# One transformer block with sparse attention on one core: order of the first loads, rows of x kept on chip, index masks of tiles 2 and 3 placed beside tiles 0 and 1, one VectorE operation in a search step

## The chip, the core and the metric

The kernel runs on one core of a Trainium2 chip. The core has five engines, each with an instruction queue of its own: TensorE (matrix products and transposes, into the accumulator banks called PSUM), VectorE, ScalarE and GpSimd (element-wise work), and SyncE, which here only issues DMA transfers between DRAM and the on-chip memory. The metric is the device time of one execution in microseconds (us). Several executions are made and their median is taken; one more is recorded by the profiler, and all rows shown come from that one.

## What is computed

The reference is one block on a sequence of 1024 tokens with 1024 features, in float32: `x = x + mixer(norm(x))`, then a cross attention to 256 memory tokens, then a squared-ReLU MLP with 4096 hidden features, each added to x. The mixer is the part that the change touches:

```python
proj = h @ w_in                      # 1024 x 1752: c_q, c_kv, k_idx, w_idx, q_nsa, kv_nsa, g_nsa
q_d = _rope(_rms_norm((c_q @ w_dsa_uq)...), pos)         # 8 heads of 64
q_i = _rope((c_q @ w_idx_q)..., pos)                     # 8 index heads of 64
...
def step(args):                      # one tile of 128 queries
    idx_score = einsum('bqhs,bqh->bqs', relu(einsum('bqhd,bsd->bqhs', qi, k_i)), wi)
    idx_score = where(pos <= t, idx_score, -inf)
    _, sel = lax.top_k(idx_score, 256)                   # 256 keys for each query
    ...                              # o_dsa: attention over the selected keys
    ...                              # o_nsa: compressed, block-selected and window attention, gated
    return concatenate([o_dsa, o_nsa])
o = lax.map(step, xs); return o @ w_out
```

With 1024 tokens there are 16 blocks of 64 and 16 are selected, so the block-selected branch is plain causal attention. For the first two query tiles all earlier keys are within the 256, so they need no index mask; tiles 2 to 7 need one each.

## The kernel before

**Stages.** The sequence is cut into 8 row tiles of 128, and the projections into two parts of four tiles (`PARTS`). The *head* projects part 0 (`project(p1, 0, ...)`). Then the *main stage* runs two streams side by side: `attend`, the attention of tiles 0 to 7, and `fill`, which first projects part 1 in the pool `p2`, then prepares the memory keys and values, then takes finished tiles through `w_out`, the cross attention (`between`) and the MLP of tiles 0 to 3 (`mlp`). A *tail* does what is left and the MLP of tiles 4 to 7 (`mlp_tail`). `together` mixes the two streams by amounts of work, in a ratio from `PACES`; tile 4 may start only when part 1 is projected. Within this program order a scheduler, run when the kernel is built, chooses the order of each engine's queue from its own estimate of times. Each engine then works its queue in that order.

**Head.** Constants come first: identity, cosine and sine tables, gains, masks, the position stack `pe` (`pe_stack`, L1143). Then `project` (L371) loads the gain of norm1 (`gain`, L338) and, tile by tile, the rows of x (L378). `norm_T` (L285) squares a tile on ScalarE with a sum, takes the root on GpSimd, scales on VectorE (L290), transposes on TensorE in groups of four (L277), and copies the result out as a high and a low half (L238, L239), or as one in part 1 (L281, L283). `gemm` (L303) loads weight groups of 256 rows (`load_w`), splits them in a high half (`whi`, L247 on ScalarE) and a low one (`wlo`, L252 on GpSimd or VectorE), and forms three products for each. In part 1 the weights are used whole (`load_whole`). The queries are staged by `stage_q` (L401): ScalarE copies them from PSUM, and each block of columns is stored to DRAM (`q`, L406), from where `q_prep` (L555) loads them for the tile in hand.

**Buffers.** Tiles come from rings of fixed length (`RINGS`, and `bufs` in `small`). A new user of a buffer waits for the last reader of the old one. `S` (L668), four buffers of 128x1024, holds the scores of attention in the pool `aw`.

**Index mask.** `index_mask` (L595) forms the index scores of tile t against all keys up to it (L604 to L613), turns each score into two 16-bit integers `hi` and `lo` and searches the 256th largest by halving, 16 steps for each half. A step has three ScalarE operations: sign of (value + bias) with its sum over the row (L639), the sign of that sum against what is needed (L640), and the new bias (L641):

```python
s.activation(mask, src, AF.Sign, bias=c, accum_out=over)
s.activation(step, over, AF.Sign, bias=nd)
s.activation(c, step, AF.Identity, scale=-0.5 * (1 << b), bias=c)
```

VectorE then reads the threshold (`tki`, L645) and forms the mask (L652 to L658). In `attend` (L830), the mask of tile t+1 is formed beside the attention of tile t; so masks 2 and 3 stand beside tiles 1 and 2.

**Attention.** For pairs of heads, `scores` (L662) forms products, masks and reduces them on VectorE (L681, L679), takes the exponential on ScalarE (L683) and scales on GpSimd (L688); `values` (L692) transposes (L698), splits the result (`ph` on ScalarE, `pl` on VectorE) and multiplies by the values.

Of the kernel before, what the change touches and what calls it, by code (L numbers as in the profile page):

```python
# [22 lines left out]
P = 128  # L23
# [11 lines left out]
NS = 4  # L35
G = 2
RINGS = {
    "p1": {"x4": 5, "st": 2, "relu": 4, "wraw": 4, "whi": 6, "wlo": 6, "c8": 4, "c4": 2, "kraw": 5, "pc": 2},
    "p2": {"x4": 3, "st": 1, "relu": 2, "whi": 4, "wlo": 4, "c8": 3, "c4": 1, "kraw": 4, "pc": 2},
# [130 lines left out]
def build(nc, tc, I, C, out):  # L170
# [8 lines left out]
    at = at_pool.__enter__()  # L179
    p1_pool, p1_psum = tc.tile_pool(name="p1", bufs=1, reuse_waits="tile"), tc.tile_pool(name="ps1", bufs=1, space=PSUM)  # L180
# [44 lines left out]

    ident = const("c_ident", [P, P])
# [58 lines left out]
    def norm_T(pool, x_t, gb, xs):  # L285
        ss = small(pool, "nss", 1)
        xn = ring(pool, "x4", [P, DM])
        s.activation(xn, x_t, AF.Square, accum_out=ss)
        r = rsqrt_of(pool, ss, DM, 1, "n")
        v.scalar_tensor_tensor(xn, x_t, r[:, 0:1], gb, op0=ALU.mult, op1=ALU.mult)  # L290
        to_T(pool, xn, xs, DM // P)
# [11 lines left out]
    def gemm(pool, xs, nk, nt, wsrc, chunks, consume):  # L303

        for ci, parts in enumerate(chunks):
            w = sum(n for _, n in parts)
            gr = []
            for k0 in range(0, nk, KG):
                kn = min(KG, nk - k0)
                srcs, o = [], 0  # L310
                for c0, n in parts:
                    srcs.append((lambda r, o=o, n=n: r[:, :, o:o + n],
                                 wsrc[k0 * P:(k0 + kn) * P, c0:c0 + n].rearrange("(k p) n -> p k n", p=P)))
                    o += n
                ws = load_w(pool, [P, kn, w], *srcs) if len(xs) == 2 else load_whole(pool, [P, kn, w], *srcs)
                gr += [[x[:, k, :] for x in ws] for k in range(kn)]
            for t in range(nt):
                pt = pst(TAGS[pool.name][0], [P, w])
                for k in range(nk):
                    if len(xs) == 1:  # L320
                        mm(pt, xs[0](t, k), gr[k][0], k == 0, k == nk - 1)
                        continue
                    wh, wl = gr[k]
                    xh, xl = xs[0](t, k), xs[1](t, k)
                    mm(pt, xh, wh, k == 0, False)
                    mm(pt, xh, wl, False, False)
                    mm(pt, xl, wh, False, k == nk - 1)
                consume(ci, t, pt)
                yield nk * (5 - len(xs)) * w / 2400.0
# [19 lines left out]
    cos = const("c_cos", [P, NT, 32], at)  # L349
    sin = const("c_sin", [P, NT, 64], at)  # L350
    qg = at.tile([P, 3, 64], F32, tag="qg", name="qg")
    nc.sync.dma_start(qg[:, 0, :], row(W["dsa_qn_g"]).to_broadcast([P, 64]))
    nc.sync.dma_start(qg[:, 1, :], row(W["nsa_qn_g"]).to_broadcast([P, 64]))
    nc.sync.dma_start(qg[:, 2, :], W["nsa_kn_g"][0:1].to_broadcast([P, 64]))
    v.tensor_scalar(qg[:, 0:2, :], qg[:, 0:2, :], -1.0, None, op0=ALU.mult)
    qgs = at.tile([P, 3, 64], F32, tag="qgs", name="qgs")
    v.tensor_copy(halves(qgs), swap(qg))
    xqg = bcast("xqg", row(W["xq_norm_g"]), 128)
    masks = const16("c_masks", [P, 640])
    window, causal = masks[:, 0:512], masks[:, 128:640]  # L360
    cmask = const16("c_cmask", [P, NT, 64])
# [9 lines left out]
    def project(pool, part, pe, st):  # L371
# [3 lines left out]
        _, xf, xt_of = xT(pool, nt, whole)  # L375
        for t in range(nt):
            x_t = ring(pool, "x4", [P, DM])
            nc.sync.dma_start(x_t, I["x"][0, (t0 + t) * P:(t0 + t + 1) * P, :])  # L378
            norm_T(pool, x_t, gb1, xt_of(t))
            yield 1.0  # L380
        cq = [ring(pool, "c8", [P, nt, 2, P], F32 if whole else F32R) for _ in xf]
# [66 lines left out]
        def w_in(chunks, first):  # L448
            return gemm(pool, xf, DM // P, nt, W["w_in"], chunks,
                        lambda ci, t, pt: consume(ci + first, t, pt))  # L450
# [4 lines left out]
        def k_prep():  # L455
            for t in range(nt):
# [31 lines left out]
        yield from w_in([[(968, 256)]], 4)  # L488
# [106 lines left out]
    def index_mask(aw, st, t):  # L595
# [29 lines left out]

        cnt, low = small(aw, "tkc", 1), small(aw, "tkf", 1)
        over, step, need = small(aw, "tko", 1), small(aw, "tks", 1), small(aw, "tkg", 2)
        th = small(aw, "tkt", 2)
        v.memset(need[:, 0:1], Wd - 2 * TOPK + 1.0)
        v.memset(th, 0.5 - 32768.0)  # L630
        for half, src in enumerate((hi, lo)):
            c, nd = th[:, half:half + 1], need[:, half:half + 1]
            if half == 1:
                v.tensor_scalar(low, th[:, 0:1], -1.0, None, op0=ALU.mult)
                v.tensor_scalar(mask, hi, low, None, op0=ALU.is_gt, op1=ALU.add, accum_out=cnt)
                v.tensor_scalar(nd, cnt, 2.0, Wd - 2 * TOPK + 1.0, op0=ALU.mult, op1=ALU.add)
                v.scalar_tensor_tensor(lo, hi, low, lo, op0=ALU.is_equal, op1=ALU.mult)
            for b in range(15, -1, -1):
                s.activation(mask, src, AF.Sign, bias=c, accum_out=over)  # L639
                s.activation(step, over, AF.Sign, bias=nd)  # L640
                s.activation(c, step, AF.Identity, scale=-0.5 * (1 << b), bias=c)  # L641
                yield 0.1
# [19 lines left out]
    def scores(aw, qh, ql, K, kt0, nk, mask, gate):  # L662
# [4 lines left out]
        for hh in range(2):  # L667
            S = small(aw, "S", L, bufs=NS)[:, :nk * P]  # L668
# [161 lines left out]
    def attend(aw, st):  # L830
# [335 lines left out]
    }  # L1166
    for kv in range(2):
# [13 lines left out]
    def fill():  # L1181
        for part in range(1, len(PARTS)):
            with tc.tile_pool(name="p2", bufs=1, reuse_waits="tile") as p2:
                yield from project(p2, part, pe, st)
# [15 lines left out]
    aw_pool.__exit__(None, None, None)  # L1200
    at_pool.__exit__(None, None, None)
# [35 lines left out]
```

## Time and profile before

| | |
|---|---|
| median of 3 runs | 1802.6 us (1800.25 to 1804.86) |
| the profiled execution | 1801.64 us |
| its span, first to last instruction | 1799.6 us |
| mean granted TensorE clock | 0.977 |
| busy: TensorE, weight loads | 1696.2 us (94%), 1457.3 (81%) |
| busy: ScalarE, VectorE, GpSimd | 1080.4 (60%), 951.0 (53%), 892.6 (50%) |
| DMA | 193.80 MB, 108 GB/s in the mean |

A row of the profile names the line of the kernel, the engine (PE is TensorE, PEld its weight loads, DVE VectorE, ACT ScalarE, POOL GpSimd, SPq SyncE's queue), the operation, and the tiles, written `out<-in`. TensorE's busy time counts a product from start to modelled end, so products that follow each other closely overlap. Idle time is put down to what ended it. The granted clock is the share of full speed that TensorE was given.

### The profile page before, as it was taken

How to read it: one execution, taken by the hardware profiler on the slowest of the kernel's cores; microseconds unless marked ns; L12 is line 12 of the kernel's file. 1: busy time of each engine (PE TensorE's matmuls, PEld its weight loads, DVE VectorE, ACT ScalarE, POOL GpSimd, SP SyncE). 2: the span in 40 equal slices, each digit the busy share in tenths (PEclk: the TensorE clock that was granted, in tenths of full speed). 3: DMA queues.
4: the chain of work that ended last, by engine and by line, in shares of the span. 5: the costliest groups of instructions: out<-in, count | busy, mean ns of one | idle time of the engine just before them, and what ended most of it. 6: DMA issues, size and time to landing. Idle time of an engine off the chain costs nothing.

```text
span 1799.6 us, 28055 instructions
## 1 busy us (share of the span) xinstructions
PE 1696.2 (94%) x9326; PEld 1457.3 (81%) x9326; DVE 951.0 (53%) x2381; ACT 1080.4 (60%) x2703; POOL 892.6 (50%) x1025
## 2 busy tenths in 40 slices
PE   5987999899989999999998999999999889999998
PEld 5986888688878777788886888887988878888887
DVE  4555757665873776365654555646524552222223
ACT  4444659797688579856896557994412543333333
POOL 2356647463551355568576576662211444444445
PEclk9997999999999999999999999999989899999999
DMA  6235221366336321222222122225375642333333
GB/s 193 74 119 150 71 76 58 109 197 177 99 107 192 98 63 42 70 71 79 61 67 83 55 71 67 67 75 187 108 245 158 209 118 84 96 94 98 96 118 107
DMA packets 176977, 193.80 MB, mean 108 GB/s; under 512 B 25664, under 2 KB 144192, under 8 KB 176832
## 3 DMA queue, kind: packets, MB, share of 16 engines
q1 hardware_dynamic: 168896, 181.52, 33.2%
q0 software_dynamic: 7936, 10.49, 2.2%
q8 instruction: 74, 1.21, 0.3%
q14 instruction: 71, 0.58, 0.1%
HBM read 170.98 MB, written 20.97 MB: 107 GB/s over the span
## 4 chain that ended last, share of the span: by engine, by line
PE 67%; DVE 9%; POOL 7%; ACT 5%; issue 5%; DMA 5%; SPq 1%; POOLq 0%; ACTq 0%; DVEq 0%
PE psD L221 48%; PE psS L221 8%; PE psPV L221 5%; PE psPT L698 4%; POOL wlo L252 3%; DMA wraw<-in_w_ff_in_dram 1%; PE psM L277 1%; ACT dmask L639 1%; DVE pl L239 1%; DVE S L681 1%; PE psPT L585 1%; ACT S L683 1%; ACT ph L238 1%; DMA qin<-q 1%; ACT whi L247 1%
## 5 line engine op out<-in xcount | busy, mean ns | idle before, releaser
L252 POOL TENSOR_TENSOR wlo<-wraw,whi 128x512 fp32r<-128x512 f32 (+1 forms) x225 | 309.5, 1380 | 266.7 <-ACT whi L247 263.0
L221 PE MATMUL psD<-whi,h 128*128 128x512 f32 x1024 | 340.7, 401 | 9.7 <-DVE b L1126 5.4
L247 ACT ACTIVATE whi<-wraw 128x512 fp32r<-128x512 f32 x321 | 200.7, 628 | 216.7 <-PE psD L221 156.4
L221 PEld LDWEIGHTS psD<-whi,h 128*128 128x128 f32 x1024 | 193.0, 190 | 55.2 <-DVE b L1126 8.8
L221 PE MATMUL psD<-xh,whi 128*128 128x512 f32 (+1 forms) x576 | 212.1, 372 | 1.2 <-ACT xh L238 0.8
L221 PE MATMUL psD<-xh,wlo 128*128 128x512 f32 (+1 forms) x576 | 212.9, 370 | 0.2 <-POOL wlo L252 0.2
L221 PE MATMUL psD<-xl,whi 128*128 128x512 f32 (+1 forms) x576 | 212.1, 370 | 0.0
L221 PE MATMUL psD<-wlo,h 128*128 128x512 f32 x512 | 203.2, 399 | 1.1 <-POOL wlo L252 1.1
L221 PE MATMUL psD<-whi,xh 128*128 128x256 f32 (+1 forms) x704 | 191.7, 353 | 4.3 <-ACT whi L247 3.2
L221 PE MATMUL psD<-wlo,xh 128*128 128x256 f32 (+1 forms) x704 | 191.3, 354 | 1.3 <-DMA wlo<-in_w_in_dram 0.7
L239 DVE TENSOR_TENSOR pl<-psPT,ph 128x512 fp32r<-128x512 f32 (+1 forms) x232 | 142.0, 620 | 80.1 <-ACT ph L238 77.4
L683 ACT ACTIVATE S<-S,mn 128x128 f32<-128x128 f32 (+7 forms) x192 | 142.6, 744 | 38.5 <-DVE mn L681 36.9
L688 POOL TENSOR_SCALAR S<-S,sums,gi 128x640 f32<-128x640 f32 (+7 forms) x128 | 107.0, 846 | 113.7 <-DVE sums L686 101.8
L252 DVE TENSOR_TENSOR wlo<-wraw,whi 128x512 fp32r<-128x512 f32 (+1 forms) x96 | 83.8, 873 | 148.8 <-ACT whi L247 148.5
L238 ACT ACTIVATE ph<-psPT 128x512 fp32r<-128x512 f32 (+1 forms) x232 | 122.7, 539 | 63.2 <-PE psPT L698 59.0
L221 PEld LDWEIGHTS psD<-wlo,xh 128*128 128x128 f32 x704 | 133.3, 194 | 13.4 <-ACT relu L416 1.2
L221 PEld LDWEIGHTS psD<-whi,xh 128*128 128x128 f32 x704 | 130.7, 194 | 14.2 <-ACT whi L247 3.6
L698 PE MATMUL psPT<-c_ident,S 128*128 128x128 f32 x816 | 131.4, 277 | 3.0 <-POOL S L688 1.6
L221 PEld LDWEIGHTS psD<-xh,whi 128*128 128x128 f32 x576 | 108.8, 189 | 19.3 <-ACT xh L238 1.6
L221 PEld LDWEIGHTS psD<-xh,wlo 128*128 128x128 f32 x576 | 109.0, 189 | 17.6 <-POOL wlo L252 0.9
L221 PEld LDWEIGHTS psD<-xl,whi 128*128 128x128 f32 x576 | 108.8, 189 | 17.1
L221 PE MATMUL psS<-K,qh 128*128 128x384 f32 (+3 forms) x288 | 112.7, 395 | 8.6 <-DVE mn L681 4.0
(282 smaller groups left out, 3863.7 us busy)
## 6 DMA issues: line engine op xcount, KB each, us to landing
wraw<-in_w_ff_in_dram SPq DMA_DIRECT2D x40, 512.0 KB, 4.0
wraw<-in_w_ff_out_dram SPq DMA_DIRECT2D x40, 512.0 KB, 3.9
wraw<-in_w_ff_in_dram SPq DMA_DIRECT2D x64, 256.0 KB, 2.7
wraw<-in_w_ff_out_dram SPq DMA_DIRECT2D x64, 256.0 KB, 2.7
whi<-in_w_out_dram SPq DMA_DIRECT2D x32, 256.0 KB, 3.6
wlo<-in_w_out_dram SPq DMA_DIRECT2D x32, 256.0 KB, 3.7
wraw<-in_w_in_dram SPq DMA_DIRECT2D x24, 256.0 KB, 3.7
q<-st SPq DMA_DIRECT2D x12, 512.0 KB, 2.6
```

The lines of the kernel that those rows point to most:

```text
L221: te.matmul(o, a, b, start=start, stop=stop)
L238: s.activation(hi, src, AF.Copy)
L239: v.tensor_tensor(lo, src, hi, op=ALU.subtract)
L247: s.activation(hi, raw, AF.Copy)
L252: (v if l == "v" else g).tensor_tensor(lo, raw, hi, op=ALU.subtract)
L277: te.transpose(pt[:, j, :], x_t[:, (c + j) * P:(c + j + 1) * P], ident)
L585: te.transpose(p2[:, h, :], qd[:, h, :, :].rearrange("p b d -> p (b d)"), ident)
L639: s.activation(mask, src, AF.Sign, bias=c, accum_out=over)
L681: v.tensor_tensor_reduce(out=dst, in0=sp, in1=m, scale=1.0, scalar=mn[:, 0:1] if i else 3e38, op0=ALU.add, op1=ALU.min, accum_out=low)
L683: s.activation(S, S, AF.Exp, bias=low, scale=-1.0, accum_out=sums[:, hh:hh + 1])
L688: g.tensor_scalar(Ss[hh], Ss[hh], sums[:, hh:hh + 1], 1.0 if gate is None else gate[:, hh:hh + 1], op0=ALU.mult, op1=ALU.mult)
L698: te.transpose(p2[:, j, hh, :], S[:, (c + j) * P:(c + j + 1) * P], ident)
```

## The change

Seven things are changed:

1. The first load is row tile 0 of x, then the identity, the gain of norm1, and in turn a group of the first weights and a row tile of x (tiles 1 to 3, into buffers of `S`). The constants and `pe_stack` follow after the four norms of the head.
2. The ring `S` moves to a pool of its own, `sp`, that is there from the start. In `k_prep` of part 0, row tiles 4 to 7 of x are loaded into its four buffers; part 1's norms read them there.
3. Part 1's norms get a higher priority in the scheduler (`SOONER`), and the ring `x4` of `p2` has 5 buffers and not 3.
4. A search step is two operations: the sign pass on ScalarE, and one on VectorE over three columns, which compares the sum and adds up the new bias. Its constants are set once, by memsets at the start (`tks`, `tko`).
5. In `attend`, mask 2 stands beside tile 0, mask 3 beside tile 1, none beside tile 2; from tile 3 on as before.
6. In `stage_q`, for two of the three kinds of queries (0 and 2), every second tile is copied by VectorE.
7. The first weights' loads are split off from `gemm` as `weights`.

```diff
-    "p2": {"x4": 3, ...
+    "p2": {"x4": 5, ...
+    sp_pool = tc.tile_pool(name="sp", bufs=1, side="right", reuse_waits="tile")
+    srow = sp_pool.__enter__()
...
+    late = {"x": ring(p1, "x4", [P, DM])}
+    nc.sync.dma_start(late["x"], I["x"][0, 0:P, :])
     ident = const("c_ident", [P, P])
...
+    def weights(pool, xs, nk, wsrc, parts):
+        w = sum(n for _, n in parts)
+        for k0 in range(0, nk, KG):
...
+            ws = load_w(pool, [P, kn, w], *srcs) if len(xs) == 2 else load_whole(pool, [P, kn, w], *srcs)
+            for k in range(kn):
+                yield [x[:, k, :] for x in ws]
...
-    def project(pool, part, pe, st):
+    def project(pool, part, late, st):
         gb1 = gain(pool, W["norm1_g"])
...
+        if not whole:
+            ws = weights(pool, xf, DM // P, W["w_in"], [(968, 256)])
+            for t in range(1, nt):
+                begun += [next(ws) for _ in range(KG)]
+                ahead[t] = small(srow, "S", L, bufs=NS)
+                nc.sync.dma_start(ahead[t], I["x"][0, t * P:(t + 1) * P, :])
+            begun += list(ws)
         for t in range(nt):
-            x_t = ring(pool, "x4", [P, DM])
-            nc.sync.dma_start(x_t, I["x"][0, (t0 + t) * P:(t0 + t + 1) * P, :])
-            norm_T(pool, x_t, gb1, xt_of(t))
+            if t0 + t in ahead:
+                x_t = ahead.pop(t0 + t)
...
+            with tc.high_priority(offset=part * SOONER):
+                norm_T(pool, x_t, gb1, xt_of(t))
...
         def stage_q(k, c, t, pt):
-            s.activation(qst[0][:, t, :], pt, AF.Copy)
+            if k != 1 and t % 2 == part:
+                v.tensor_copy(qst[0][:, t, :], pt)
+            else:
+                s.activation(qst[0][:, t, :], pt, AF.Copy)
...
+                if part == 0:
+                    ahead[4 + t] = small(srow, "S", L, bufs=NS)
+                    tc.keep_in_program_order(load_x(ahead[4 + t], 4 + t))
...
-                s.activation(mask, src, AF.Sign, bias=c, accum_out=over)
-                s.activation(step, over, AF.Sign, bias=nd)
-                s.activation(c, step, AF.Identity, scale=-0.5 * (1 << b), bias=c)
+                i = 15 - b
+                s.activation(mask, src, AF.Sign, bias=tks[:, i, 1:2], accum_out=over[:, 0:1])
+                v.scalar_tensor_tensor(small(aw, "tkj", 3), over, nd, tks[:, i, :], op0=ALU.is_gt, op1=ALU.mult,
+                                       accum_out=tks[:, i + 1, 1:2] if b else th[:, half:half + 1])
...
-            S = small(aw, "S", L, bufs=NS)[:, :nk * P]
+            S = small(srow, "S", L, bufs=NS)[:, :nk * P]
...
-            side = index_mask(aw, st, t + 1) if 2 <= t + 1 < NT else iter(())
-            for w in beside(of_tile(t), tile_work(t), side, 8 * 0.15 * (t + 2) + 3.4):
+            n = {0: 2, 1: 3, 2: NT}.get(t, t + 1)
+            side = index_mask(aw, st, n) if n < NT else iter(())
+            for w in beside(of_tile(t), tile_work(t), side, 8 * 0.15 * (n + 1) + 3.4):
...
+    v.memset(st["tko"], BIG)
+    v.memset(st["tks"][:, 0, 1:2], 0.5 - 32768.0)
+    for i in range(16):
+        v.memset(st["tks"][:, i, 0:1], -1.0 * (1 << (15 - i)))
+        v.memset(st["tks"][:, i, 2:3], 0.5 * (1 << (15 - i)))
...
-    pe = pe_stack()
-    drain(project(p1, 0, pe, st))
+    head = project(p1, 0, late, st)
+    for _ in range(PARTS[0][1]):
+        next(head)
+    cos = const("c_cos", [P, NT, 32], at)
...
+    late["pe"] = pe_stack()
+    drain(head)
```

`over` has three columns: the sum, and two of a large constant, so that the comparison gives 0 or 1 for the first and 1 for the others; the products with the row of `tks` (minus a step, the old bias, half a step) are added up to the new bias.

More of the change, by code (lines that the diff above doesn't have):

```diff
@@ L368, in build, with load_x @@
     xo_dr = [dr.tile([P, 512], F32, tag=f"xo{t}", name=f"xo{t}") for t in range(NT)]
-    def project(pool, part, pe, st):
+    ahead = {0: late["x"]}
+    def load_x(x_t, t):
+        return nc.sync.dma_start(x_t, I["x"][0, t * P:(t + 1) * P, :])
+    def project(pool, part, late, st):
         t0, nt = PARTS[part]
@@ L626, in index_mask @@
         cnt, low = small(aw, "tkc", 1), small(aw, "tkf", 1)
-        over, step, need = small(aw, "tko", 1), small(aw, "tks", 1), small(aw, "tkg", 2)
+        over, tks, need = st["tko"], st["tks"], small(aw, "tkg", 2)
         th = small(aw, "tkt", 2)
-        v.memset(need[:, 0:1], Wd - 2 * TOPK + 1.0)
-        v.memset(th, 0.5 - 32768.0)
+        v.memset(need[:, 0:1], 2.0 * TOPK - 1.0 - Wd)
         for half, src in enumerate((hi, lo)):
-            c, nd = th[:, half:half + 1], need[:, half:half + 1]
+            nd = need[:, half:half + 1]
             if half == 1:
@@ L1183, in fill @@
             with tc.tile_pool(name="p2", bufs=1, reuse_waits="tile") as p2:
-                yield from project(p2, part, pe, st)
+                yield from project(p2, part, late, st)
             projected.append(part)
```

67 lines of the change are left out of this document (36 added, 31 removed).

## The prediction

> **What bounds the kernel now.** I read the page first, then busy time by windows, then the timeline of the two places where TensorE stands still, then who waits for whom. From the page: the span, TensorE's busy tenths, and its granted clock (40 slices of 45 us).
>
> ```profile
> span 1799.6 us, 28055 instructions
> ...
> PE   5987999899989999999998999999999889999998
> ...
> PEclk9997999999999999999999999999989899999999
> ```
>
> TensorE is at 9 nearly everywhere. The lower digits stand at the start (5), in slice 4 (7, clock 7), near 320 to 360 us, and in some later slices with a clock of 8. So time can come only out of those places. Next, windows; the columns are busy us of TensorE, its weight loads, VectorE, ScalarE, GpSimd (instructions in brackets), granted clock, DMA share, GB/s.
>
> ```profile
> 0.00:20.00 20.00, 2.35 (x10) 1.85 (x10) 3.65 (x11) 3.41 (x5) 1.56 (x9) 1.00 0.58 174
> 20.00:40.00 20.00, 17.35 (x127) 17.07 (x128) 14.96 (x22) 14.67 (x30) 6.75 (x7) 1.00 0.80 225
> 160.00:180.00 20.00, 19.06 (x108) 16.75 (x107) 12.50 (x57) 12.46 (x48) 14.57 (x31) 0.83 0.39 98
> 300.00:320.00 20.00, 19.80 (x114) 17.29 (x113) 15.29 (x40) 18.94 (x63) 14.69 (x18) 1.00 0.21 70
> 320.00:340.00 20.00, 15.61 (x75) 11.32 (x73) 10.32 (x27) 15.93 (x53) 7.34 (x12) 1.00 0.25 91
> 340.00:360.00 20.00, 17.31 (x96) 14.39 (x96) 16.83 (x55) 14.74 (x44) 6.57 (x10) 1.00 0.47 156
> 360.00:380.00 20.00, 17.92 (x88) 15.44 (x89) 13.93 (x39) 18.92 (x55) 11.31 (x18) 0.83 0.78 244
> 960.00:980.00 20.00, 18.83 (x80) 14.49 (x78) 8.05 (x11) 14.73 (x32) 14.94 (x13) 1.00 0.33 98
> 980.00:1000.00 20.00, 15.61 (x51) 11.67 (x52) 13.62 (x27) 6.43 (x15) 9.73 (x10) 0.74 0.08 27
> 258.00:1218.00 960.00, 918.60 (x4975) 777.21 (x4974) 591.13 (x1541) 742.38 (x1908) 552.09 (x640) 0.99 0.30 91
> ```
>
> The first 20 us hold 2.35 us of TensorE work. From 300 to 380 us TensorE misses 0.20 + 4.39 + 2.69 + 2.08 = 9.4 us, and a clock of 0.83 costs another 0.17 x 20 = 3.4. There ScalarE is close to full (18.94 and 18.92 of 20) at both ends. From 960 to 1000 us the loss is 1.17 + 4.39 idle and 0.26 x 20 = 5.2 of clock, 10.8 in all. Over 258 to 1218 us, the stretch in which the index masks are searched, ScalarE is busy 77% and VectorE 62%.
>
> **The change part by part.** *Head loads.* Columns: start, duration, engine, line, operation, and in brackets the wait before it.
>
> ```profile
> 0.73 0.38 SPq L197 DMA_DIRECT2D c_ident<-in_c_ident_dram  x1
> ...
> 7.77 0.35 SPq L378 DMA_DIRECT2D x<-in_x_dram  x1
> ...
> 13.83 1.06 ACT L288 ACTIVATE x<-x 128x1024 f32<-128x1024 f32 x1 [1.95 <-DMA x<-in_x_dram]
> ...
> 15.97 1.28 DVE L290 SCALAR_TENSOR_TENSOR x<-x,nr,x 128x1024 f32<-128x1024 f32 x1 [0.74 <-POOL nr L234]
> ...
> 17.31 1.97 PE L277 MATMUL psM<-c_ident,x 128*128 128x128 f32 x8 [5.69 <-DVE x L290]
> ...
> 22.48 0.58 PE L221 MATMUL psD<-whi,xh 128*128 128x256 f32 x1 [3.21 <-ACT whi L247]
> ```
>
> Row tile 0 of x is the 13th issue, 7.77 - 0.73 = 7.04 us after the first, so one issue takes 0.59. Its load is used at 13.83; VectorE scales it 2.14 later; the transposes start 1.34 after that. Now it is issued first (0.73), the gain third (about 1.9). How long each takes to land at an empty queue is bounded by these rows (median us from issue to landing, last column):
>
> ```profile
> x<-in_x_dram SPq DMA_DIRECT2D x4, 512.0 KB, 5.4
> ...
> x<-in_norm_g_dram SPq DMA_DIRECT2D x1, 512.0 KB, 5.3
> ...
> c_sin<-in_c_sin_dram SPq DMA_DIRECT2D x1, 256.0 KB, 2.8
> ```
>
> With 5.4 for x and 5.3 for the gain, VectorE starts at max(0.73 + 5.4 + 2.14, 1.9 + 5.3) = 8.3 and TensorE at 9.6; with 2.8 for both, at max(5.7, 4.7) = 5.7 and 7.0. I take the gain at 5.3 and x faster, as nothing stands ahead of x: 7.2 and 8.5. That is 17.31 - 8.5 = 8.8 earlier (7.7 to 10.3). The first product then follows after 5.2 us as before, or somewhat later, because ScalarE squares tile 1 and splits the first weights in one queue: I take **-8**, with 5 to 10 as bounds.
>
> The Trainium skill ("DMA: Bandwidth & Descriptors", section "Anatomy of one DMA") gives a fixed 2.0 us plus bytes over 436 GB/s; for c_sin that is an estimate of 2.6, and the trace has 2.8. By it x and the gain would land after an estimated 3.2 us each, the transposes would start at 7.4 and the sum would be 1.1 us lower; its fit is for another issuing path, so I keep the rows.
>
> What carries this on: after 22.48 TensorE is without a hole (17.35 of 20 to 40 us, the rest lies before that product), so a head moved forward stays moved, if later weights keep up. 21 constant loads, formerly ahead of x, now stand between the fourth weight group and the next chunk's weights: 21 x 0.59 = 12.4 us of SyncE, ending near 20 us; four tiles' products need about as long. If that cover fails, 3 us go back. The 35 one-column memsets run while VectorE waits for x anyway.
>
> *Handoff to part 1.* TensorE's last head product, then the second half's first work:
>
> ```profile
> 130.78 0.28 PE L221 MATMUL psD<-whi,c 128*128 128x256 f32 x1
> ...
> 131.91 0.38 SPq L340 DMA_DIRECT2D x<-in_norm_g_dram  x1
> 132.40 0.73 SPq L378 DMA_DIRECT2D x<-in_x_dram  x1
> 133.22 0.41 SPq L559 DMA_DIRECT2D qin<-q  x1
> ...
> 138.38 1.06 ACT L288 ACTIVATE x<-x 128x1024 f32<-128x1024 f32 x1 [6.91 <-DMA x<-in_x_dram]
> ...
> 140.39 1.28 DVE L290 SCALAR_TENSOR_TENSOR x<-x,nr,x 128x1024 f32<-128x1024 f32 x1
> ...
> 141.82 1.09 PE L277 MATMUL psM<-c_ident,x 128*128 128x128 f32 x4 [10.76 <-DVE x L290]
> ...
> 145.44 0.80 PE L221 MATMUL psD<-wlo,xh 128*128 128x256 f32 x1 [0.73 <-DMA wlo<-in_w_in_dram]
> ```
>
> The head ends near 131.06. Load of x's row tile 4, square, scaling and transposes follow, so TensorE stands 10.76 us. Now tiles 4 to 7 lie on chip; their four loads are issued earlier, between weight loads. The squares can follow ScalarE's last q copy at once. What comes late next is the gain of norm1, still issued behind the last q store at 131.91:
>
> ```profile
> x<-in_norm_g_dram SPq DMA_DIRECT2D x1, 512.0 KB, 4.7
> ```
>
> It lands at 136.6 (4.7), scaling starts there and not at 140.39: 3.8 earlier. The weights for 145.44 are no earlier, except for one issue less; but the transposes of tiles 5 to 7 come into that gap. If the gain takes 2.8, 5.7 are won; if weights set everything, 1. I take **-4**, and nothing for the clock, as about 7 us of standstill remain.
>
> One wait is added: the four S buffers hold x's tiles 4 to 7, so the first scores of tile 0 wait for VectorE's scaling of those rows, with the exponentials queued behind it. The four scalings take 4 x 1.28 us from 136.6; the first q for those scores is loaded only at 133.22 and still has its norm and rotation to go through: no cost.
>
> *Masks 2 and 3 earlier, smaller steps.* Each of 192 search steps had two one-column ScalarE operations, which go (busy us in total, then mean ns):
>
> ```profile
> L641 ACT ACTIVATE tkt<-tks,tkt 128x1 f32<-128x1 f32 x192 | 55.7, 290 | 3.0
> L640 ACT ACTIVATE tks<-tko,tkg 128x1 f32<-128x1 f32 x192 | 55.5, 289 | 2.3
> ```
>
> 55.7 + 55.5 = 111 us leave ScalarE; 742 of 960 falls to 631 (66%). VectorE gets 192 operations of 3 columns with an accumulator, a form absent here. Nearest rows:
>
> ```profile
> L681 DVE DVE_READ_ACCUMULATOR2_ANT mn<- 128x1 f32 x256 | 20.6, 80 | 0.0
> ...
> L746 DVE TENSOR_SCALAR csum<-csum 128x2 f32<-128x2 f32 x32 | 8.4, 264 | 11.6 <-ACT cS L744 11.3
> ...
> L232 DVE TENSOR_SCALAR nms<-nss 128x1 f32<-128x1 f32 x26 | 3.9, 149 | 17.5 <-ACT xh L296 10.2 <-ACT x L288 7.3
> ```
>
> From below 149 + 80 = 229 ns, from above 264 + 80 = 344; by its width it is nearest to the lower, so 0.23 x 192 = 44 us (66 at most): VectorE rises from 62 to about 66 or 68%, no bound. 16 of 48 q copies also move there. The sign passes run till now over these times (min, median, max ns, first and last start):
>
> ```profile
> L639 ACT ACTIVATE dmask<-tkh,tkt x96: 598/878/1151, 258.2 to 1154.4; 128x384 bf16<-128x384 uint16 x16, 128x512 bf16<-128x512 uint16 x16, 128x640 bf16<-128x640 uint16 x16, 128x768 bf16<-128x768 uint16 x16
> ```
>
> Masks 2 and 3, the first of them from 258 us on, move beside tiles 0 and 1, where ScalarE has room (12.46 of 20 at 160). So the stretch from 300 to 380 loses 64 steps of ScalarE work in front of TensorE. Its whole loss is 12.8; gain 0 to 12.8, taken as half, **-6**, since part of it is the start of other chains.
>
> *The search's end.* One row of VectorE's timeline:
>
> ```profile
> 971.74 0.62 DVE L645 TENSOR_SCALAR tki<-tkt 128x2 uint32<-128x2 f32 x1 [17.19 <-ACT tkt L641]
> ```
>
> VectorE stood 17.2 us for the last step of a mask, in the stretch that then loses 10.8. A search shorter by 32 x 0.58 = 18.6 us of ScalarE covers that. Gain 0 to 10.8, taken **-6**.
>
> *The new coupling.* Each step now goes ScalarE, VectorE, ScalarE; behind a step on VectorE wait the score reductions and the subtraction pl, for which TensorE's value products wait (total us, times, longest):
>
> ```profile
> DVE pl L239 <- ACT ph L238: 77.4, 70, 4.1
> ```
>
> ```profile
> PE psPV L221 <- DVE pl L239: 3.5, 8, 0.7
> ```
>
> VectorE waited 77.4 us for pl's input and TensorE paid 3.5: a rate of 0.05. At the long wait, 17.2 cost up to 10.8: a rate of 0.63. If the 192 steps wait about as much as pl does, 77 us, this costs 4 to 49; TensorE has projection or MLP products between, so I take the lower, **+4**.
>
> Sum: -8 - 4 - 6 - 6 + 4 = **-20**. The profiled execution took 1801.64 us (span 1799.6 and 2.0 around it), the median of the runs is 1802.6, 1.0 above. 1781.6 by the profiled one; forecast **1781**.
>
> **The rivals.** *Lock step (slower).* The searches hold VectorE: a step placed too early in its order waits out a sign pass on ScalarE, and the scores behind it come late. For it speaks the 17.2 us wait, which shows that the built order can expect a search too early; against it, that the chain gets shorter. With 77 us of waits it decides from a rate of 24/77 = 0.31 on; at 0.45 it costs 35: 1801.6 - 24 + 35 = 1813. The Trainium skill ("TensorE: Matmul & The Clock Gate", section "Architectural detail") says that ScalarE's and VectorE's queues are strictly first in, first out, which speaks for this rival; the trace agrees in that nothing passed the waiting tki for 17.2 us.
>
> *Hidden relief.* ScalarE's work was off the path and the losses at 300 to 380 and 960 to 1000 come back at other places, because dependent chains start there; head and handoff remain, less 3 for the constants: 1801.6 - 12 + 3 + 4 = 1797. For it: TensorE is 918.6 of 960 busy, whatever ScalarE does.
>
> *Full relief.* Both losses vanish and the head starts at its early bound: -10 - 5 - 12.8 - 10.8 + 4 = -35, 1767. Against it: each of those windows has more than one wait.
>
> *The loads don't do what they say.* Weights and gain compete with x's rows, the first product gains only 5 and later weights give 3 back: -2 in place of -8, 1801.6 - 14 = 1788; it lies inside the forecast's range and has 0.10 of its chance.
>
> **How the numbers follow.** The forecast with its near neighbours (1771 to 1792) 0.50, full relief 0.17, hidden relief 0.20, lock step 0.13. About 0.3% (5.4 us) can be told from no change: 1797.2 and 1808. Full relief and forecast are faster; hidden relief stands at the bound, 0.12 of it faster and 0.08 same; lock step is slower. So 0.79, 0.08, 0.13. The range, 1762 to 1803, leaves lock step and little else out; the likeliest case's own is 1771 to 1792.
>
> **What would show it.** Head right: first transposes near 8.5, first product by 14, first 20 us with over 8 us of TensorE. Handoff right: a standstill near 7 us that ends with the gain, not with x. Relief right: more than 18.5 of 20 in each window of the same work (then some 15 us earlier) and no wait of over 5 us of VectorE for ScalarE. Lock step: VectorE's waits for tko over 80 us in total and TensorE idle behind score reductions. A head that ends less than 5 us earlier, or TensorE's idle time in the masks' stretch above the present 41.4, would make the forecast wrong.

## The result and the profile after

| | before | after |
|---|---|---|
| median of six runs each, us | 1802.71 (1797.77 to 1804.86) | 1811.62 (1806.83 to 1812.68) |
| ratio, 95% interval | 1 | 1.0045 (1.0031 to 1.0059) |
| profiled execution, us (its span) | 1801.64 (1799.6) | 1806.83 (1805.1) |

The kernel became slower by 0.45%, some 8 us, where 21 us less were forecast. The profiled execution is the fastest of the six, so its trace holds some 5 us of the loss (1806.83 against 1801.64). First the page of the changed kernel, with the lines that answer to those of before.

```profile
span 1805.1 us, 28037 instructions
...
PE 1699.0 (94%) x9326; PEld 1458.2 (81%) x9326; DVE 1005.5 (56%) x2809; ACT 984.9 (55%) x2303; POOL 887.3 (49%) x1025
...
PE   7989999999989988999999999999999889999998
...
DVE  4556779865885786656765667536234452222223
ACT  5444777853784688457955598555123443333333
...
PEclk9999999899999999999999999999999899999999
```

TensorE's slices 1 and 4, the head's start and the handoff, are fuller than before (7 and 9, where they had 5 and 7), but 8s are new in slices 15 and 16 (632 to 722 us). VectorE now is busier than ScalarE. In windows (columns as before):

```profile
0.00:20.00 20.00, 10.51 (x62) 9.55 (x63) 10.58 (x52) 10.92 (x19) 4.87 (x10) 1.00 0.67 230
20.00:40.00 20.00, 17.02 (x131) 16.65 (x130) 9.31 (x21) 9.46 (x24) 5.09 (x8) 0.91 0.85 195
258.00:1218.00 960.00, 912.08 (x4965) 773.31 (x4963) 644.66 (x1890) 638.12 (x1465) 552.04 (x651) 0.98 0.29 88
660.00:690.00 30.00, 21.46 (x123) 17.85 (x121) 25.44 (x79) 26.32 (x61) 18.56 (x23) 0.90 0.12 33
```

The first 20 us hold 10.51 us of TensorE work, not 2.35. In the stretch of the searches TensorE is idle 960 - 912.08 = 47.9 us, where it was 41.4, and this although ScalarE's load there fell from 742 to 638 us (the prediction had 631) and VectorE's rose only to 67%. The changed kernel searches earlier, from 189 to 1125 us; there TensorE is idle 47.4 us. In the stretch from 660 to 690, inside a search, TensorE has only 21.46 of 30 and a clock of 0.90, while neither VectorE (25.44) nor ScalarE (26.32) is full: none of the three fills this stretch.

Head and handoff, from the timeline (start, duration, engine, line, operation, wait ahead of it):

```profile
7.30 1.28 DVE L295 SCALAR_TENSOR_TENSOR x<-x,nr,x 128x1024 f32<-128x1024 f32 x1 [1.60 <-DMA x<-in_norm_g_dram]
...
8.64 1.97 PE L282 MATMUL psM<-c_ident,x 128*128 128x128 f32 x8 [8.64 <-DVE x L295]
...
11.21 0.58 PE L224 MATMUL psD<-whi,xh 128*128 128x256 f32 x1 [0.60 <-ACT xh L243]
...
23.95 0.49 DVE L207 CAST c_masks<-x 128x640 bf16<-128x640 f32 x1 [3.69 <-DMA x<-in_c_masks_dram]
...
24.36 0.68 DVE L244 TENSOR_TENSOR xl<-psM,xh 128x512 fp32r<-128x512 f32 x1
...
25.10 0.98 PE L282 MATMUL psM<-c_ident,x 128*128 128x128 f32 x4 [2.98 <-DVE xl L244]
...
131.61 2.48 DVE L295 SCALAR_TENSOR_TENSOR x<-S,nr,x 128x1024 f32<-128x1024 f32 x2 [2.92 <-DMA x<-in_norm_g_dram]
...
133.05 1.08 PE L282 MATMUL psM<-c_ident,x 128*128 128x128 f32 x4 [7.03 <-DVE x L295]
...
138.35 2.08 PE L224 MATMUL psD<-wlo,xh 128*128 128x256 f32 x4 [2.42 <-DMA wlo<-in_w_in_dram]
```

The first transposes start at 8.64 (forecast 8.5) and the first product at 11.21 (forecast by 14). They end the standstill of the start with VectorE's scaling, which itself waited for the gain, as the prediction had it. A hole of 2.98 us at 22.1 is new, and the rows show why: VectorE stood 3.69 us for the constant `c_masks`, one of the loads that now come behind x and the first weights, and `xl`, for which TensorE waited, stood behind it in VectorE's queue. At the handoff TensorE stands 7.03 us and not 10.76, and what ends it is again the gain of norm1 (2.92 us of VectorE's wait); 2.42 us for weights follow. The head's last product ended near 131.06 before and near 126.02 now, so 5.0 us were won by then, and 3.7 more at the handoff. As the first product came 11.3 us earlier (22.48 before), the head gave 6.2 back on the way: 3.0 in the hole, and an estimated 1.8 by the granted clock of 0.91 from 20 to 40 us (0.09 x 20), where it was 1.00.

So 8.8 us are ahead at part 1's first transposes (141.82 and 133.05). In these two executions the rest takes 14.3 us longer, 1672.0 us for 1657.7. Where? The view of waits gives what TensorE waited for (total us, times, longest). Of the kernel before:

```profile
PE psD L221 <- DVE b L1126: 5.4, 8, 1.5
...
PE psM L277 <- DVE xl L239: 4.8, 3, 3.8
...
PE psS L221 <- DVE mn L681: 4.1, 7, 1.0
...
PE psD L221 <- DVE b L894: 0.3, 1, 0.3
```

Of the changed kernel:

```profile
PE psM L282 <- DVE xl L244: 11.2, 5, 3.8
PE psD L224 <- DVE b L1150: 7.1, 9, 1.7
PE psS L224 <- DVE mn L704: 6.9, 8, 2.1
PE psPV L224 <- DVE pl L244: 5.2, 7, 1.4
...
PE psD L224 <- DVE b L918: 3.6, 3, 2.2
...
PE psS L224 <- DVE iql L244: 2.4, 3, 2.0
...
PE psM L495 <- DVE K L498: 2.2, 1, 2.2
```

These are the waits for VectorE that grew or are new; the largest, for `x`, is 15.9 us and was 16.6. Summed over all of TensorE's rows in the timeline, by the engine that ended the wait, the waits for VectorE rose from 52.7 to 73.0 us.

The start and the handoff are in these sums. From part 1's first transposes on, TensorE's busy time stayed (1587.6 us before, 1586.4 now) and its idle time rose from 70.1 to 85.6 us, which is the whole loss. There the waits for VectorE rose from 33.9 to 53.2 us and those for transfers from 5.1 to 10.0, while those for ScalarE fell from 22.0 to 14.4 and those for GpSimd from 5.1 to 3.7. Not all of it lies beside the searches: after the attention, which ends near 1304.9 before and 1289.5 now, TensorE is idle 29.4 us and was 22.3.

### The profile page after: what moved, and what is told of

Read it like the earlier page. It is cut to its first block, busy times and chain, and to the rows that moved or that the text cites. A ratio compares the mean times of both kernels' runs of the same rounds, so it can differ in the third digit from the quotient of the medians.

```text
span 1805.1 us, 28037 instructions
## 1 busy us (share of the span) xinstructions
PE 1699.0 (94%) x9326; PEld 1458.2 (81%) x9326; DVE 1005.5 (56%) x2809; ACT 984.9 (55%) x2303; POOL 887.3 (49%) x1025
## 4 chain that ended last, share of the span: by engine, by line
PE 53%; DVE 7%; ACT 5%; issue 3%; DMA 2%; POOL 1%; SPq 0%; DVEq 0%; POOLq 0%; ACTq 0%
PE psD L224 39%; PE psS L224 7%; PE psPV L224 3%; PE psPT L721 2%; ACT dmask L662 2%; DMA relu<-xo 1%; DVE tkj L663 1%; ACT whi L252 1%; DMA whi<-in_w_out_dram 1%; PE psM L282 1%; ACT S L706 1%; ACT ph L243 1%; DVE pl L244 1%; DVE S L704 0%; POOL wlo L257 0%
```

## The experiments

Sixteen kernels were run, each beside the kernel before on the same chip; the ratios are to those runs. 0.1% is 1.8 us.

### Each part by itself, or taken back

Three theories were open: that the new chain ScalarE, VectorE, ScalarE costs the time (1), that the new order of everything else does (2), and that the masks crowd the first tiles (3). The order is not written in the kernel: a scheduler makes it when the kernel is built, from an estimate of every instruction's time. After the change with the step taken back, `after_old_step`:

```diff
-                s.activation(mask, src, AF.Sign, bias=tks[:, i, 1:2], accum_out=over[:, 0:1])
-                v.scalar_tensor_tensor(small(aw, "tkj", 3), over, nd, tks[:, i, :], ...
+                s.activation(mask, src, AF.Sign, bias=c, accum_out=over)
+                s.activation(step, over, AF.Sign, bias=nd)
+                s.activation(c, step, AF.Identity, scale=-0.5 * (1 << b), bias=c)
```

> The changed kernel with the search step put back to three operations on ScalarE; everything else stays. Theory 1, the step costs: in the changed kernel VectorE waited 68.2 us for sign passes and ScalarE 31.7 us for steps, and without this coupling the kernel falls to 1785 to 1792 us, about the forecast. Theory 2, reordering: the step is near worth nothing by itself (its 30 us of saved search time are worth what TensorE's idle time shows, some 0 to 6 us), the loss comes from where the new order puts its stalls and from the work left for the time after attention: 1800 to 1815 us, and the attention ends later than in the changed kernel (1289.5 us). Theory 3, the masks placed beside tiles 0 and 1 crowd ScalarE: with three more operations on ScalarE per step this gets worse, 1812 to 1825 us.

Measured: 1802.5 us, ratio 0.9993 (0.9983 to 1.0004). The kernel before with the new step alone (the same diff the other way):

> The kernel of before with only the search step as one VectorE operation. Theory 1 (the coupling of ScalarE and VectorE costs 15 to 25 us): 1815 to 1825 us. Theory 2 (reordering): 1795 to 1806 us, with the wait of 17.2 us for tki at the end of a search shorter, and stalls moved to other places. Theory 3 (masks): 1795 to 1803 us.

Measured: 1827.0 us, 1.0133 (1.0118 to 1.0148). The kernel before with the masks moved alone:

```diff
-            side = index_mask(aw, st, t + 1) if 2 <= t + 1 < NT else iter(())
+            n = {0: 2, 1: 3, 2: NT}.get(t, t + 1)
+            side = index_mask(aw, st, n) if n < NT else iter(())
```

> The kernel of before with only the masks of tiles 2 and 3 moved beside tiles 0 and 1. Theory 1 (the step costs, the masks do as forecast): 1794 to 1802 us. Theory 2 (reordering): 1797 to 1808 us; tiles 0 and 1 longer, tiles 2 and 3 shorter by the same within 4 us. Theory 3 (the masks crowd ScalarE while tiles 0 and 1 need it): 1808 to 1818 us.

Measured: 1808.1 us, 1.0028 (1.0017 to 1.0040). The kernel before with the loads alone (parts 1, 2, 3 and 7 of the change, of which these are lines):

```diff
+    late = {"x": ring(p1, "x4", [P, DM])}
+    nc.sync.dma_start(late["x"], I["x"][0, 0:P, :])
...
+            with tc.high_priority(offset=part * SOONER):
+                norm_T(pool, x_t, gb1, xt_of(t))
...
+                    ahead[4 + t] = small(srow, "S", L, bufs=NS)
+                    tc.keep_in_program_order(load_x(ahead[4 + t], 4 + t))
```

> The kernel of before with the new order of loads, x's later rows on chip, norms of part 1 sooner, the S pool and the ring of five; without the new search step, the moved masks and the copies of q on VectorE. Theory 1 (step costs): the loads give what they gave in the changed kernel, 5 us in the head and 3 to 4 us at the handoff: 1793 to 1796 us. Theory 2 (reordering): the same gain up to part 1, then given back in the attention or after it: 1798 to 1806 us. Theory 3 (masks): as theory 1.

Measured: 1821.9 us, 1.0099 (1.0082 to 1.0115). And the changed kernel with the masks back in their old places:

> The changed kernel with the masks of tiles 2 and 3 back beside tiles 1 and 2, scheduler free. By theory 3 (the masks crowd the first tiles, +4.5 us when moved alone in the kernel of before): 1804 to 1809 us. By theory 2 the amount can't be foretold from the part moved alone: anything from 1800 to 1835 us, with its stalls at other places than in the changed kernel.

Measured: 1815.7 us, 1.0064 (1.0051 to 1.0077).

`after_old_step` lies in theory 2's range, and its attention ends near 1306 us, later than the changed kernel's 1289.5, as that theory asked. The new step alone and the loads alone are slower than every range given for them, and 1808.1 stands at the edge that theories 2 and 3 share, so it decides nothing. Theory 3 falls with the last run: it asked for 1804 to 1809 us, and with the masks put back the changed kernel is no faster (1.0064 and 1.0045, with intervals that overlap). And the parts don't add up. Alone, loads, masks and step cost 0.99 + 0.28 + 1.33 = 2.60%; together, with the copies of q, 0.45%. The loads, which win 9 us by 140 us in the trace of the changed kernel, lose 18 by the end when they are alone, and the step costs 24 us on the kernel before but 9 on the rest of the change. No fixed price per part gives these numbers. The largest stall of the loads alone, from the timeline of `before_loads` (ScalarE and TensorE):

```profile
342.85 0.29 ACT L661 ACTIVATE tkt<-tks,tkt 128x1 f32<-128x1 f32 x1
...
347.77 1.06 ACT L301 ACTIVATE xh<-b 128x1024 f32<-128x1024 f32 x1 [4.63 <-DMA b<-in_mem_dram]
...
348.82 0.58 ACT L625 ACTIVATE ir<-psS 128x512 f32<-128x512 f32 x1
...
349.45 0.69 PE L224 MATMUL psS<-K,qh 128*128 128x384 f32 x1 [10.03 <-ACT ir L625]
```

ScalarE stands 4.63 us for a row of the second input (`mem`), whose norm the scheduler had put there; behind it in ScalarE's queue stands a relu of index scores, `ir`, whose product TensorE had finished before 339.4, as it did nothing from then to 349.45. It starts when the norm's operation has ended, and TensorE, which needs its bank, stood 10.03 us, in 4.63 of which ScalarE did nothing. The Trainium skill ("TensorE: Matmul & The Clock Gate", section "Architectural detail") has ScalarE's queue as strictly first in, first out; these rows agree, as `ir` didn't pass in the 4.63 us. The edit itself touches neither operation.

### The same instructions in another order

The next kernels hold the order. At the end of the build, each instruction of a queue is chained to the one ahead of it in a list, which was read from another build; instructions of the search step that the list hasn't got (ScalarE's two small ones, or VectorE's one, and the memsets) are left to the scheduler. No operation is added or taken away by it: with the new step alone the engines have the same numbers of operations free and held (9326 on TensorE, 2793 on VectorE, 2319 on ScalarE, 1025 on GpSimd); only the instructions around them, such as waits, differ (28038 and 28089 in all). What the chaining costs by itself was not measured: the kernel before was not timed with its own list. Together with the new step it costs 3 us (the first run below).

```diff
+    for name, packed in ORDER.items():
+        steps = json.loads(zlib.decompress(base64.b85decode(packed)))
...
+            tc.add_manual_dep(ins[k], last, mybir.DependencyInfo(mybir.DependencyClass.NoSync, mybir.DependencyReason.DATA),
+                              reason="order")
+            last = ins[k].name
```

The new step in the order of the kernel before:

> The kernel of before with the search step as one VectorE operation, and every other instruction of all five queues kept in the order that it has in the kernel of before (without this the new step alone moved 5364 of the 8458 TensorE instructions to another place, and took 1827.0 us). Theory 1, the coupling of ScalarE and VectorE costs time: still 1815 to 1830 us. Theory 2, the order that the scheduler made around the new step costs it: 1793 to 1806 us, that is the time of before, with the shorter search a gain of 0 to 10 us.

Measured: 1806.3 us, 1.0018 (1.0005 to 1.0031). The old step in the order that the scheduler had made for the new one:

> The counterpart: the kernel of before with its old search step of three ScalarE operations, and all other instructions in the order that the scheduler made for the new step (the one that took 1827.0 us). The instructions are those of the kernel of before, only their places differ. Theory 1: without the coupling 1798 to 1808 us. Theory 2: 1818 to 1835 us, since the stalls of that order stay.

Measured: 1906.5 us, 1.0574 (1.0553 to 1.0596). The same on the changed kernel:

> The changed kernel with the search step put back to three ScalarE operations and everything else held in the changed kernel's own order (left to the scheduler, the same instructions took 1802.5 us). Theory 1: the coupling gone, 1790 to 1803 us. Theory 2: the order stays and its stalls with it, 1808 to 1825 us, no better than the changed kernel's 1811.6.

Measured: 1897.5 us, 1.0532 (1.0511 to 1.0553).

The first of them decides: with the order held, the new step costs 3 us and not 24 (1806.3 is just above theory 2's range). The two lists, with the old order and the new, differ at 5364 of TensorE's 8458 places, 1429 of VectorE's 2011 and 1204 of ScalarE's 1794. The other two overshoot both theories. Their instructions are those of the kernel before (1803) and of `after_old_step` (1802.5), and the order alone makes them 95 to 103 us slower. It fits that an order built for a short search places the work behind it earlier, and pays when each of the 192 steps is longer; this reason is argued, the size is measured.

That the coupling isn't the price shows in VectorE's own waits for the sign passes, which *Lock step* made its sign (from the views of waits of `before_new_step`, 1827.0 us, and of `new_step_old_order`, 1806.3 us):

```profile
DVE tkj L640 <- ACT dmask L639: 73.6, 88, 3.6
```

```profile
DVE tkj L797 <- ACT dmask L796: 96.7, 96, 4.0
```

The kernel with the longer waits is 21 us faster. The other half of the chain, ScalarE's waits for the steps, hardly differs: 28.3 and 29.6 us.

### Which queue's order

The new step on the kernel before again, with the list of one or two queues kept and the others left out, for instance:

```diff
 ORDER = {
     "PE": (
...
-    "Activation": (
...
-    "DVE": (
...
```

TensorE's alone:

> The kernel of before with the new search step, only TensorE's order held as in before; the other four queues are left to the scheduler. If the time is lost by TensorE's order: 1802 to 1810 us, as with all five queues held (1806.3). If it is lost by what stands ahead of what on ScalarE and VectorE: 1818 to 1830 us.

Measured: 1824.3 us, 1.0113 (1.0096 to 1.0130). ScalarE's alone, VectorE's alone, and both:

> The kernel of before with the new search step, only ScalarE's order held as in before. If what stands around the sign passes on ScalarE loses the 20 us (with TensorE's order alone held it was 1824.3, with all five 1806.3): 1803 to 1812 us. If ScalarE's order isn't it: 1818 to 1830 us.

> The same, only VectorE's order held (its new steps are free among the old instructions). If VectorE's order loses the time: 1803 to 1812 us; if not: 1818 to 1830 us.

> The same, ScalarE's and VectorE's orders both held, the other three queues free. If the loss sits in the order of these two together: 1803 to 1810 us; if it needs the order of the transfers or of GpSimd too: 1812 to 1830 us.

Measured: 1821.9 us, 1.0104 (1.0083 to 1.0125); 1812.6 us, 1.0055 (1.0037 to 1.0073); 1807.0 us, 1.0025 (1.0014 to 1.0037).

Of the 1.15% between the free and the held order (1.0133 and 1.0018), TensorE's list gives back 0.20, ScalarE's 0.29, VectorE's 0.78, and VectorE's and ScalarE's together 1.08. TensorE's 0.20 is within the noise of the two runs, and ScalarE's 0.29 barely outside it; 1812.6 us lies just above the range for VectorE's order. The loss sits in what stands ahead of what on VectorE, and next on ScalarE.

### The loads in the order of before, and the whole change in a held order

The loads alone again, with the queues held in the order of before from the first scores of tile 0 on; the head, the handoff and the first scores' surroundings stay free, since they are what the loads change (held are 7480 of TensorE's instructions, 1815 of VectorE's, 1610 of ScalarE's, 934 of GpSimd's and 634 of SyncE's). Then with the new step as well, with the 192 sign passes free and with them held (the expectation's 384 counts each with the instruction that reads its sum):

> The kernel of before with the loads part alone (loads in order of need, x's rows on chip, norms of part 1 sooner), as in the run that took 1821.9 us when the scheduler was free; here all queues keep, from the first scores of tile 0 on (7480 of the 8458 TensorE instructions), the order that they have in the kernel of before. Theory 2, the order costs the time: the 8 to 9 us won by the end of the handoff (head 5, standstill 3.7) stay won, 1793 to 1798 us. Theory 1 as widened after the run of the loads alone, the loads themselves cost time later (more transfers in the head, a fuller on-chip memory): 1808 to 1825 us.

> The same with the new search step as well, order of before from the first scores on. Theory 2: the step was worth -1 to +4 us in the order of before (1806.3 against 1804.4 us), so 1793 to 1800 us. Theory 1: 1812 to 1830 us.

> The kernel with the loads part and the new search step, in the order of before from the first scores on, this time with ScalarE's 384 sign passes held in their old places too (in the run that took 1808.0 us they were left to the scheduler). Theory 2 (places cost): 1793 to 1798 us, the loads' gain whole, the step worth -1 to +4. If the coupling itself costs the 14 us: 1804 to 1812 us.

Measured: 1793.7 us, 0.9946 (0.9933 to 0.9959); 1808.0 us, 1.0031 (1.0018 to 1.0045); 1800.9 us, 0.9983 (0.9970 to 0.9995). The first meets theory 2; the other two lie between the ranges of their theories, and the places of the sign passes alone are worth 0.48%. Finally the changed kernel whole, in the order that the scheduler had made for `after_old_step`:

> The changed kernel whole, new step included, with every other instruction of all five queues in the order that the scheduler made for it with the old step (that one took 1802.5 us). If the step itself costs what it cost in the held orders before (+3 to +7 us): 1805 to 1810 us, little better than the changed kernel's 1811.6; if the changed kernel lost by its order: 1799 to 1806 us.

Measured: 1797.6 us, 0.9976 (0.9963 to 0.9988), a little below both ranges.

`loads_old_order` beats both kernels by 0.54% and 0.99%. It is the kernel that took 1821.9 us with a free scheduler, so its order was worth 28 us. Its handoff, from the timeline of the profiled execution (1799.3 us):

```profile
132.71 1.09 PE L432 MATMUL psM<-c_ident,x 128*128 128x128 f32 x4 [7.07 <-DVE x L445]
...
138.29 2.07 PE L374 MATMUL psD<-wlo,xh 128*128 128x256 f32 x4 [2.69 <-DMA wlo<-in_w_in_dram]
```

It has the same 7.07 us of standstill as the changed kernel, and keeps what it won; the stall of 10.03 us is gone, and no wait of TensorE from 300 to 390 us is over 1.9 us. Held to the last sign pass, the step costs the loads 0.37% (7 us); on the kernel before it cost 0.18%, and in the changed kernel (0.9976 against 0.9993) it gains 0.17%, hardly more than the noise. Between -3 and +7 us, then, depending on its surroundings.

`after_held` has every instruction of the changed kernel, new step and all, in another order, and is 0.69% (12 us) faster than it. Its waits of TensorE for VectorE:

```profile
PE psPV L385 <- DVE pl L405: 8.5, 10, 1.5
...
PE psD L385 <- DVE b L1311: 5.4, 8, 1.5
PE psM L443 <- DVE xl L405: 5.4, 4, 3.8
PE psS L385 <- DVE mn L865: 4.6, 8, 1.0
...
PE psS L385 <- DVE iql L405: 1.4, 3, 0.7
...
PE psD L385 <- DVE b L1079: 0.5, 2, 0.3
```

All waits of TensorE for VectorE together are 56.2 us by its rows, against 73.0 in the changed kernel and 52.7 before. Its VectorE waits longer for the sign passes than the changed kernel's (96.1 and 68.2 us, from these two rows of the views of waits):

```profile
DVE tkj L824 <- ACT dmask L823: 96.1, 102, 5.2
```

```profile
DVE tkj L663 <- ACT dmask L662: 68.2, 95, 2.3
```

What such a wait for VectorE looks like in the changed kernel, from its timeline (VectorE and TensorE):

```profile
684.18 0.99 DVE L599 TENSOR_TENSOR qd<-qta,qtb 128x256 f32<-128x256 f32 x1
684.20 0.57 ACT L243 ACTIVATE iqh<-psPT 128x512 fp32r<-128x512 f32 x1
...
684.83 0.68 PE L224 MATMUL psS<-K,iqh 128*128 128x512 f32 x2
685.10 0.21 DVE L663 SCALAR_TENSOR_TENSOR tkj<-tko,tkg,tks 128x3 f32<-128x3 f32 x1
...
685.24 0.74 DVE L305 SCALAR_TENSOR_TENSOR relu<-b,nr,h 128x512 f32<-128x512 f32 x1
...
685.96 0.88 DVE L597 TENSOR_TENSOR qtb<-qin,c_sin 128x256 f32<-128x256 f32 x1
686.76 0.68 DVE L244 TENSOR_TENSOR iql<-psPT,iqh 128x512 fp32r<-128x512 f32 x1
...
687.50 1.11 PE L224 MATMUL psS<-K,iql 128*128 128x512 f32 x2 [1.99 <-DVE iql L244]
```

ScalarE had written `iqh`, which `iql` needs, at 684.77 (start 684.20, 0.57). VectorE was not waiting for anything: it did a rotation, a step, a norm of the fill (0.74) and another rotation (0.88) first, and then the split that TensorE stood 1.99 us for.

## Why the prediction was wrong

**Head loads, -8 (5 to 10).** Mechanism right, size off: transposes at 8.64 for 8.5, but the head's end moved by 5.0, the lower bound. The sentence that failed is "a head moved forward stays moved, if later weights keep up". It wasn't a weight that came late but a constant, `c_masks`, through VectorE's queue; the price named for such a case, 3 us, is the 2.98 of the hole. The gain was issued at 1.65 and VectorE started at 7.30, so it took at most 5.65 us, near the 5.3 of the row of before. Tile 0 of x, issued first at 0.74, was used at 4.36, 3.6 us later. The Trainium skill's sum ("DMA: Bandwidth & Descriptors", section "Anatomy of one DMA") had given an estimate of 3.2 for both; that was nearer for x, and the row of the trace was the better guide for the gain.

**Handoff, -4.** Right in size and in cause: 3.7 us, ended by the gain. With the order held, the loads part, which holds both terms, is worth 0.54%, 9.7 us (7.4 to 12.1), against 12.

**Relief from masks 2 and 3, -6, and the search's end, -6.** Neither came out. The stretch that was to lose its stalls has 47.9 us of idle TensorE for 41.4. Masks moved alone cost 5 us (0.28%), but with a free scheduler; what they are worth in a held order was not measured. A shorter search in the old order gained nothing (+3 us): ScalarE's relief of 104 us there was off the path. The 17.2 us wait of VectorE did vanish, and no wait for a sign pass is over 2.3 us. From part 1's first transposes on, TensorE's waits for ScalarE did fall by 7.6 us, but those for VectorE rose by 19.3. A wait that is read in one queue was booked as a gain in another, on the ground that both lie in the same 40 us.

**The new coupling, +4.** In a held order the step cost -3 to +7 us, so the size was near. VectorE's waits for the sign passes came to 68.2 us for the forecast 77. *Lock step* asked for over 80, and over 80 stands in fast kernels (96.7 us in 1806.3, 96.1 in 1797.6) as in a slow one (89.3 in the 1821.9 of ScalarE's list): this wait doesn't set the time.

**The step that failed** is the sum itself: each edit was costed with all other instructions where they were, and what their new places cost was put at nothing, without a reason. Such a sum needs an order that stays. Here the step alone changed 5364 of TensorE's 8458 places, though the edit touches none of these instructions. In the changed kernel, what VectorE did first cost TensorE 19.3 us more of waiting from part 1 on (33.9 to 53.2), which no term of the sum contained and which ate the 8.8 us won before. In another order the same change comes to 1797.6 us.

That this is the time of *hidden relief* (1797) is partly luck: the relief is hidden indeed, but 1797.6 belongs to one order among many, the step there gained 3 us where that rival charged 4, and the loads in a held order gave 9.7 us for that rival's 9. *Lock step* has luck too: its 1813 is near the measured 1811.6, and it named the right pair of engines and the queues in order, but its time came from long waits for the sign passes, and these were 68.2 us, below its own sign of 80.

Two slips of the prediction change nothing: the memsets are 34 and not 35, and as the median lay 1.0 us above the profiled execution, its sum gives 1782.6 and not 1781.

What stays open: what the copies of q on VectorE cost (not tried alone), what the masks' new places are worth in a held order, and by which of the scheduler's estimates VectorE's order goes wrong.

## What to carry to other kernels

Where a build step makes the order, an edit has two prices, its own and that of the new order. Hold the old order to measure the first; here the second was up to 28 us, for edits that in a held order were worth -10 to +7. Before forecasting a sum of small gains from such a change, count how many instructions move on each queue, and give the range the width that a reordering has shown. And when a version wins in one stretch and loses elsewhere, try it in the old order before dropping it: the loads alone went from 1% slower to 0.5% faster.

## What the runs showed of the hardware

VectorE's step of three columns took 348 ns in the mean, over the forecast's upper end of 264 without its readback, but the mean hides a long tail. The view of its line gives minimum, median and maximum, and the timeline the longest one with GpSimd's work beside it:

```profile
L663 DVE SCALAR_TENSOR_TENSOR tkj<-tko,tkg,tks x192: 194/223/2131, 189.4 to 1124.3; 128x3 f32<-128x3 f32 x192
```

```profile
519.29 1.73 POOL L711 TENSOR_SCALAR S<-S,sums,gi 128x640 f32<-128x640 f32 x2
...
519.61 2.13 DVE L663 SCALAR_TENSOR_TENSOR tkj<-tko,tkg,tks 128x3 f32<-128x3 f32 x1
...
520.99 0.71 POOL L600 TENSOR_TENSOR qd<-qta,qtb 128x256 f32<-128x256 f32 x1
...
521.78 0.83 ACT L662 ACTIVATE dmask<-tkh,tks 128x640 bf16<-128x640 uint16 x1 [2.54 <-DVE tkj L663]
```

Of the 192 steps 131 took under 260 ns, 49 of them beside GpSimd. All 61 longer ones ran while GpSimd was working, the longest beside three GpSimd operations (from 519.29 to 521.70), with ScalarE's next sign pass waiting 2.54 us for it. The Trainium skill ("SBUF — State Buffer", section "Who interferes with whom") says that a VectorE instruction with two inputs in on-chip memory contends with a GpSimd instruction that reads there; the step has two, and these rows agree. At the median of 223 ns the 192 steps would be 42.8 us and not 66.9, so 24 us of VectorE's time went to the longer ones.

The other surprise is a size: the same operations, with the same data and the old step in both, took 1803 or 1906 us, 5.7% apart, by their order in the queues.
